# Second channel product: products in another order, scale and residual ahead of the last units, output turns into four banks

## The chip, the cores and the metric

The kernel runs on one core of a Trainium2 chip. The metric is device time in microseconds (us) of one execution of the whole program; the median of three runs is 2000.34 us (1999.61 to 2003.00). Engines are named as in the profile: PE is TensorE, PEld its weight loads, DVE is VectorE, ACT is ScalarE, POOL is GpSimd, SP is SyncE, which here only issues DMAs.

## The reference, cut to what matters

One decoder block on 512 tokens of width 2048: attention and gating heads, an output projection with a residual, then the channel MLP, and a last RMSNorm. The change lies in the last two lines.

```python
def rmsnorm(x, g):
    y = x * lax.rsqrt(jnp.mean(x * x, axis=-1, keepdims=True) + EPS)
    return y * g
...
x = x + jnp.einsum('bse,ed->bsd', merged, w_out[l])
h2 = rmsnorm(x, norm_ffn_g[l])
a = jax.nn.relu(jnp.einsum('bsd,df->bsf', h2, w_ff1[l]))   # 512 x 2048 by 2048 x 8192
x = x + jnp.einsum('bsf,fd->bsd', a * a, w_ff2[l])         # 512 x 8192 by 8192 x 2048
return rmsnorm(x, norm_final_g)
```

Since relu squared is homogeneous, the row scale of `h2` is left out of the first product and put in behind the second: the last sum is `r2 * (a * a) @ w_ff2 + x2`, where `r2` is the squared inverse root for each token and `x2` the residual.

## The kernel before, in words

Every product of two float32 matrices is computed as three matmuls in a reduced format: each operand is split into a high part (ACT, a cast into `wh`) and a low part (DVE, `wl` = operand minus `wh`), and PE adds high by high, high by low and low by high. Both channel products are blocked by two and use seven products of block sums in place of eight (the Strassen-Winograd scheme, P1 to P7).

The second channel product is `second_product`. It runs over 16 units, `(kc, n)`: eight depths `kc` of 1024, and two halves `n` of the columns. A unit has seven products; a product has two halves `h` (a group, 12 matmuls of 128x512), so a unit is 14 groups and 168 matmuls and the whole is 2688. The left factors `fac` were made by the first product, stored in DRAM and read back once per `kc` (line 877). The right factors are four blocks of `w2` per unit (B11, B12, B21, B22, each in two halves `raw`, line 870), from which DVE forms block sums in place: `B11 += B12` for P5 (line 887), `B11 += B22` for P6 (889), `B12 += B22` for P7 (891), and behind P6 `B21 += B11` for P4 (898). `prepare` (880) makes the sum, the cast (895) and the low part (896) of one group, two groups ahead of PE; `wh` and `wl` have three buffers, so a cast can start when PE has left the group three back. A block's next load is issued when its last use has been prepared (`follows`).

The products add up in PSUM where the scheme allows: P1, P6, P7 and P4 go one after the other into the pair of banks X, P2 into Y, P5 and P3 into Z. In between, the running sum in X or Z is wanted as well, so ACT copies X after P1 (`k1`), Z after P5 (`k5`) and X after P6 (`k2`) into SBUF (`keep`, line 916), a pair of copies each, and PE may not add to a bank before its copy is done. After P2, P7 and P3 DVE adds bank and kept copy into the accumulators `acc` (`add_kept`, lines 924 and 925: two additions for each half of the tokens), after P4 the bank alone (line 909).

The order of products in a unit is `usual` (P1, P2, P5, P6, P7, P3, P4); the last unit has `final`, with P4 in a pair of banks W. In the last two units (`kc` = 7) `settle` (953) scales each finished accumulator by `r2` and adds the residual (DVE, line 957), and ACT squares it and sums (959). `finish` (961), run for the first 256 tokens after P3 and for the others after P4, makes the inverse root (a short chain DVE, POOL, lines 964, 122, 123), scales the accumulators (DVE 972, ACT 970), turns them by PE into PSUM banks (981; four 128x128 turns a bank), and from each bank ACT (990) and DVE (988) take one half each, times the norm's gain, into `y`, which SP stores (991), 512 KB a time.

The order of PE's work is the order in which the code is written. That of the other engines is made by a scheduler, as is the place of a DMA in SP's queue; each queue then runs strictly in its order.

Of the kernel before, what the change touches and what calls it, by code (L numbers as in the profile page):

```python
# [8 lines left out]
F32 = mybir.dt.float32  # L9
# [25 lines left out]
def hybrid_block(ctx, tc, xT, win, wf_in, wout, w1, w2, cols_in, ln_in, ws_in, out):  # L35
# [28 lines left out]
    def mm(name):  # L64
        return ps_mm.tile([P, 512], F32, tag="mm", name=name)
# [587 lines left out]
    A11, A12, A22, S1, S2, S3, S4 = range(NF)  # L653
    P1, P2, P3, P4, P5, P6, P7 = range(1, 8)
    left = {P1: A11, P2: A12, P3: S4, P4: A22, P5: S1, P6: S2, P7: S3}
    usual = (P1, P2, P5, P6, P7, P3, P4)
    first = (P5, P1, P6, P2, P7, P4, P3)
    fac = [dram.tile([NF, P, 1024], F32, name=f"fac{u}") for u in range(NU)]
    stage = {}
# [172 lines left out]
    def second_product():  # L832
# [47 lines left out]
        def prepare(i):  # L880
            x, p, h = groups[i]

            def raw(b):
                return raws[x, b, h]

            if p == P5:
                nc.vector.tensor_tensor(raw(B11), raw(B11), raw(B12), ALU.add)
            if p == P6:
                nc.vector.tensor_tensor(raw(B11), raw(B11), raw(B22), ALU.add)
            if p == P7:  # L890
                nc.vector.tensor_tensor(raw(B12), raw(B12), raw(B22), ALU.add)
            s = raw(source[p])
            wh = w2_pool.tile([P, 1024], F32R, tag="wh", name=f"wh{x}_{p}_{h}")
            wl = w2_pool.tile([P, 1024], F32R, tag="wl", name=f"wl{x}_{p}_{h}")
            nc.scalar.copy(wh, s)  # L895
            nc.vector.tensor_tensor(wl, s, f(wh), ALU.subtract)  # L896
            if p == P6:
                nc.vector.tensor_tensor(raw(B21), raw(B21), raw(B11), ALU.add)
            ready[i] = wh, wl
            if p in follows:  # L900
                load(x + 1, follows[p], h)

        def take(bank, how):
            for t in range(2):
                how(t, bank[t])
# [10 lines left out]
                nc.scalar.copy(s[t], ps)  # L916
            return s, how

        def add_kept(c, s, first, bank, ps_op, s_op):
# [33 lines left out]
        def settle(th, q, x2l):  # L953
            a = acc[th, q]
            for t in range(2):
                tb = 2 * th + t
                nc.vector.scalar_tensor_tensor(a[:, t, :], a[:, t, :], r2[:, tb:tb + 1], x2l[:, t, :],  # L957
                                               ALU.mult, ALU.add)
                nc.scalar.activation(x2l[:, t, :], a[:, t, :], AF.Square, accum_out=sums[:, tb, q:q + 1])

        def finish(th):
            tbs = slice(2 * th, 2 * th + 2)
            r = rl[:, tbs]
            nc.vector.tensor_reduce(r, sums[:, tbs, :], axis=AX.X, op=ALU.add)
            inv_root(r, r, D, 2)
            for q in range(4):
                for t in range(2):
                    a, rt = acc[th, q][:, t, :], rl[:, 2 * th + t:2 * th + t + 1]
                    if t:
                        nc.scalar.activation(a, a, AF.Copy, scale=rt)  # L970
                    else:
                        nc.vector.tensor_scalar(a, a, rt, None, ALU.mult)
            yield 3
            for q in range(4):
                y = y_pool.tile([P, 4, 256], F32, tag="y", name=f"y{th}{q}")
                for jj in range(2):
                    ps = mm(f"pt{th}{q}{jj}")
                    for j in range(2):
                        for t in range(2):
                            c = 2 * jj + j  # L980
                            nc.tensor.transpose(ps[:, j * 256 + t * P:j * 256 + (t + 1) * P],
                                                acc[th, q][:, t, c * P:(c + 1) * P], ident)
                    for j in range(2):
                        k = 4 * q + 2 * jj + j
                        g = cols[:, G_LAST + k:G_LAST + k + 1]
                        d = y[:, 2 * jj + j, :]
                        if j:
                            nc.vector.tensor_scalar(d, ps[:, 256:512], g, None, ALU.mult)
                        else:
                            nc.scalar.activation(d, ps[:, 0:256], AF.Copy, scale=g)  # L990
                nc.sync.dma_start(out=out[q * 512:(q + 1) * 512, th * 256:(th + 1) * 256].rearrange("(m p) c -> p m c", p=P),
                                  in_=y)
# [5 lines left out]
        def evacuate(x, p):  # L998
            kc, n = units2[x]
            first, end = kc == 0, kc == LAST  # L1000
            o = order_of(x)
            name = f"{x}_{p}"
            lo, hi = 2 * n, 2 * n + 1
            X, Y, Z = banks["X"], banks.get("Y"), banks.get("Z")

            def done(c):
                if end:
                    settle(*c, x2_for[c])

            if p == P1:  # L1010
                kept[1], how = keep(f"k1_{x}")
                take(X, how)
                if end:
                    for c in ((0, lo), (0, hi), (1, hi), (1, lo)):
                        x2_for[c] = load_x2(*c)
            elif p == P2:
                add_kept((0, lo), kept[1], first, Y, ALU.add, ALU.add)
                done((0, lo))
            elif p == P6:
                kept[2], how = keep(f"k2_{x}")  # L1020
                take(X, how)
            elif p == P5:
                kept[5], how = keep(f"k5_{x}")
                take(Z, how)
            elif p == P7:
                add_kept((1, hi), kept[5], first, X, ALU.subtract, ALU.add)
                if o is final:
                    take(X, add_ps((1, lo)))
                done((1, hi))
            elif p == P3:  # L1030
                add_kept((0, hi), kept[2], first, Z, ALU.add, ALU.subtract)
                done((0, hi))
                if o is final:
# [22 lines left out]
        for i, (x, p, h) in enumerate(groups):  # L1056
# [131 lines left out]
```

## Time and profile before

| | us |
|---|---|
| median of three runs | 2000.34 |
| the profiled execution, as timed | 2002.97 |
| its span | 2001.3 |
| PE busy | 1966.3 (98%) |
| PEld busy | 1721.9 (86%) |
| DVE busy | 1597.4 (80%) |
| ACT busy | 1051.7 (53%) |

The span is the stretch from the first to the last instruction of the profiled execution; 1.7 us of the timed 2002.97 lie outside it. PE's granted clock was at its higher level (2.4 GHz) for nearly the whole span. The second channel product begins on PE at 1353.5 us and ends at 1983.5; what follows is the last norm, the turns and the stores. A matmul's end is modelled, so that PE counts as busy through short waits; its weight loads (PEld) and the distance between the starts of two matmuls show them.

### The profile page before, as it was taken

Reading aid. Unit: us, or ns where it says so; the run is one execution under the profiler, and the core shown is the slowest. Engines: PE = TensorE matmul, PEld = TensorE weight load, DVE = VectorE, ACT = ScalarE, POOL = GpSimd, SP = SyncE. Lnnn points to the kernel's source line nnn. Section 1 sums busy time; section 2 is a strip of 40 time slices with the busy share of each in tenths; the row PEclk is TensorE's granted clock in tenths of the full one; section 3 lists DMA queues with packets and bytes.
Section 4 is the critical chain, followed back from the end, with each engine's and each line's share of the span. In section 5 each row is a group of like instructions: output and inputs, shape, how many; then the busy total and the mean of one; then the engine's idle time right before and its main releaser. Section 6 shows DMA issues by size and latency. Waiting matters only on the chain.

```text
span 2001.3 us, 30641 instructions
## 1 busy us (share of the span) xinstructions
PE 1966.3 (98%) x11288; PEld 1721.9 (86%) x11288; DVE 1597.4 (80%) x2400; ACT 1051.7 (53%) x1692; POOL 84.1 (4%) x84
## 2 busy tenths in 40 slices
PE   9999999999999999999999999999999999999996
PEld 6888887888787899999999999997888888888875
DVE  7567567677667789888888888888888988998897
ACT  6344334445423566666666666666554444444455
POOL 5000001100121000000000000000000000000000
PEclk9999999999999999999999999999999999999999
DMA  6465565667766789986677667778855656646632
GB/s 217 152 198 167 186 193 174 200 211 242 247 204 199 249 270 307 334 270 201 207 243 238 209 203 236 240 263 314 328 198 202 231 165 224 241 137 237 245 128 84
DMA packets 226406, 439.91 MB, mean 220 GB/s; under 512 B 18896, under 2 KB 96848, under 8 KB 226128
## 3 DMA queue, kind: packets, MB, share of 16 engines
q1 hardware_dynamic: 225568, 436.09, 64.6%
q8 instruction: 88, 1.44, 0.3%
q10 hardware_dynamic: 432, 1.35, 0.2%
q0 software_dynamic: 256, 0.52, 0.1%
q14 instruction: 62, 0.51, 0.1%
HBM read 337.22 MB, written 100.66 MB: 219 GB/s over the span
## 4 chain that ended last, share of the span: by engine, by line
PE 58%; DVE 5%; DMA 3%; issue 1%; ACT 1%; SPq 0%; POOLq 0%; POOL 0%; DVEq 0%; ACTq 0%
PE q L802 28%; PE bX L1078 16%; PE bZ L1078 7%; PE bY L1078 4%; DMA b<-in_w_dram 1%; DVE wl L896 1%; PE ps_og L152 1%; PE ps_og L150 1%; PE ps_og L151 1%; DVE fl L734 1%; DMA x2d<-x2t 1%; DMA x2l<-x2d 0%; DVE acc L957 0%; DVE acc L924 0%; DMA t1d<-b 0%
## 5 line engine op out<-in xcount | busy, mean ns | idle before, releaser
L802 PE MATMUL q<-form,fh 128*128 128x256 f32 x3584 | 647.4, 283 | 1.0 <-DVE x L616 1.0
L802 PEld LDWEIGHTS q<-form,fh 128*128 128x128 f32 x3584 | 559.4, 192 | 1.4 <-DVE x L616 1.0
L802 PE MATMUL q<-form,fl 128*128 128x256 f32 x1792 | 508.6, 284 | 2.1 <-DVE fl L734 1.9
L895 ACT CAST wh<-raw 128x1024 fp32r<-128x1024 f32 x224 | 234.4, 1054 | 221.4 <-PE bX L1078 121.3
L802 PEld LDWEIGHTS q<-form,fl 128*128 128x128 f32 x1792 | 343.9, 192 | 4.1 <-DVE fl L734 3.4
L896 DVE TENSOR_TENSOR wl<-raw,wh 128x1024 fp32r<-128x1024 f32 x224 | 271.2, 1223 | 72.6 <-ACT wh L895 71.7
L1078 PE MATMUL bX<-wh,fac 128*128 128x512 f32 x1008 | 322.3, 393 | 4.3 <-ACT k_wl L916 2.1
L1078 PEld LDWEIGHTS bX<-wh,fac 128*128 128x128 f32 x1008 | 190.0, 188 | 52.3 <-ACT k_wh L916 6.8
L734 DVE TENSOR_TENSOR fl<-t,fh 128x512 fp32r<-128x512 f32 x256 | 176.2, 690 | 68.0 <-ACT fh L733 66.8
L733 ACT CAST fh<-t 128x512 fp32r<-128x512 f32 x256 | 158.2, 618 | 117.0 <-PE q L802 78.8
L1078 PE MATMUL bX<-wl,fac 128*128 128x512 f32 x504 | 198.8, 394 | 1.9 <-DVE wl L896 1.9
L1078 PE MATMUL bZ<-wh,fac 128*128 128x512 f32 x512 | 162.8, 389 | 0.0
L1078 PEld LDWEIGHTS bX<-wl,fac 128*128 128x128 f32 x504 | 95.0, 188 | 25.5 <-DVE wl L896 7.0
L1078 PEld LDWEIGHTS bZ<-wh,fac 128*128 128x128 f32 x512 | 96.1, 188 | 20.0
L733 ACT CAST fh<-r 128x512 fp32r<-128x512 f32 x128 | 79.1, 618 | 46.0 <-PE q L802 39.9
L150 PE MATMUL ps_qk<-xh,wh_qk 128*128 128x512 f32 x256 | 101.6, 397 | 0.0
L152 PE MATMUL ps_qk<-xh,wl_qk 128*128 128x512 f32 x256 | 100.0, 391 | 0.0
L151 PE MATMUL ps_qk<-xl,wh_qk 128*128 128x512 f32 x256 | 99.8, 390 | 0.0
L1078 PE MATMUL bZ<-wl,fac 128*128 128x512 f32 x256 | 99.6, 389 | 0.0
L734 DVE TENSOR_TENSOR fl<-r,fh 128x512 fp32r<-128x512 f32 x128 | 88.2, 689 | 10.1 <-ACT fh L733 9.4
L162 ACT ACTIVATE wh_qk<-raw_qk,cols 128x512 fp32r<-128x512 f32 x64 | 46.3, 724 | 94.7 <-PE ps_qk L151 62.9
L163 DVE SCALAR_TENSOR_TENSOR wl_qk<-raw_qk,cols,wh_qk 128x512 fp32r<-128x512 f32 x64 | 47.7, 750 | 59.0 <-ACT wh_qk L162 58.9
(618 smaller groups left out, 3559.1 us busy)
## 6 DMA issues: line engine op xcount, KB each, us to landing
b<-in_w_dram SPq DMA_DIRECT2D x256, 256.0 KB, 4.4
raw<-in_w_dram SPq DMA_DIRECT2D x128, 512.0 KB, 4.9
fac<-fac SPq DMA_DIRECT2D x112, 512.0 KB, 6.3
r<-in_w_dram SPq DMA_DIRECT2D x64, 512.0 KB, 5.6
fac<-fc SPq DMA_DIRECT2D x48, 512.0 KB, 3.9
raw_qk<-in_win_dram SPq DMA_DIRECT2D x32, 512.0 KB, 3.8
t1d<-b SPq DMA_DIRECT2D x64, 256.0 KB, 2.2
t3d<-b SPq DMA_DIRECT2D x64, 256.0 KB, 2.4
```

The lines of the kernel that those rows point to most:

```text
L150: nc.tensor.matmul(ps, lhsT=ah, rhs=bh, start=start, stop=False)
L151: nc.tensor.matmul(ps, lhsT=ah, rhs=bl, start=False, stop=False)
L152: nc.tensor.matmul(ps, lhsT=al, rhs=bh, start=False, stop=stop)
L162: nc.scalar.activation(wh, raw, AF.Copy, scale=g)
L163: nc.vector.scalar_tensor_tensor(wl, raw, g, f(wh), ALU.mult, ALU.subtract)
L733: nc.scalar.copy(pairs(wh), b[p])
L734: nc.vector.tensor_tensor(pairs(wl), b[p], pairs(f(wh)), ALU.subtract)
L802: nc.tensor.matmul(d, lhsT=l[:, c], rhs=r, start=j == 0 and q == 0 and m == 0 and w == 0, stop=j == 3 and q == 1 and w == 2, skip_group_ch ...
L895: nc.scalar.copy(wh, s)
L896: nc.vector.tensor_tensor(wl, s, f(wh), ALU.subtract)
L1078: nc.tensor.matmul(banks[chain][t], lhsT=l, rhs=r, start=start and w == 0, stop=stop and w == 2, skip_group_check=True)
```

## The change

- `usual` and `final` put P2 behind P6 instead of ahead of P5. The sum `B21 += B11` moves behind P2, and B11's next load with it. The first loads follow the new order.
- `settle` is gone. `settle_task`, started with P1 of each of the two last units, loads the four residual tiles and, before the unit's products are added, makes each accumulator `acc * r2 + x2`. The products of the two last units are then added by `add_scaled`, one instruction each, `acc + r2 * source` (or with `nr2`, which is minus `r2`). The squares (`squares`) go to ACT, and the last of the 16 to DVE as a product with a running sum.
- In `finish` the eight banks of turns of each token half alternate between the matmul pool and two banks of their own, and each bank has one reader: DVE with one instruction over both gains, or ACT with two. DVE takes five of the eight scalings in place of four. The second token half's `y` lies in buffers of `raw`, and its last 512 KB are stored in two parts.

In the rows below a name is tile, unit, product, half and a running number: `wl8_6_1` is the low part for unit 8, P6, second half; `raw8_0_1` is B11's second half (blocks 0 to 3 are B11, B12, B21, B22).

DVE, a middle unit (8), from the low part of P5's second half to that of P7's first; before:

```order
L896 TENSOR_TENSOR wl8_5_1_17744<-raw8_0_1_17492,wh8_5_1_17743 128x1024
L924 TENSOR_TENSOR acc00_15277<-acc00_15277,bY8_0_17728 128x512
L924 TENSOR_TENSOR acc00_15277<-acc00_15277,bY8_1_17729 128x512
L925 TENSOR_TENSOR acc00_15277<-acc00_15277,k1_8_wh_17719 128x512
L925 TENSOR_TENSOR acc00_15277<-acc00_15277,k1_8_wl_17720 128x512
L896 TENSOR_TENSOR wl8_6_0_17769<-raw8_0_0_17470,wh8_6_0_17768 128x1024
L898 TENSOR_TENSOR raw8_2_0_17605<-raw8_2_0_17605,raw8_0_0_17470 128x1024
L889 TENSOR_TENSOR raw8_0_1_17492<-raw8_0_1_17492,raw8_3_1_17580 128x1024
L898 TENSOR_TENSOR raw8_2_1_17623<-raw8_2_1_17623,raw8_0_1_17492 128x1024
L896 TENSOR_TENSOR wl8_6_1_17791<-raw8_0_1_17492,wh8_6_1_17790 128x1024
L896 TENSOR_TENSOR wl8_7_0_17815<-raw8_1_0_17518,wh8_7_0_17814 128x1024
```

and now:

```order
L896 TENSOR_TENSOR wl8_5_1_17707<-raw8_0_1_17491,wh8_5_1_17706 128x1024
L896 TENSOR_TENSOR wl8_6_0_17728<-raw8_0_0_17472,wh8_6_0_17727 128x1024
L889 TENSOR_TENSOR raw8_0_1_17491<-raw8_0_1_17491,raw8_3_1_17581 128x1024
L891 TENSOR_TENSOR raw8_1_1_17538<-raw8_1_1_17538,raw8_3_1_17581 128x1024
L896 TENSOR_TENSOR wl8_6_1_17747<-raw8_0_1_17491,wh8_6_1_17746 128x1024
L896 TENSOR_TENSOR wl8_2_0_17771<-raw8_2_0_17606,wh8_2_0_17770 128x1024
L898 TENSOR_TENSOR raw8_2_0_17606<-raw8_2_0_17606,raw8_0_0_17472 128x1024
L896 TENSOR_TENSOR wl8_2_1_17790<-raw8_2_1_17624,wh8_2_1_17789 128x1024
L898 TENSOR_TENSOR raw8_2_1_17624<-raw8_2_1_17624,raw8_0_1_17491 128x1024
L896 TENSOR_TENSOR wl8_7_0_17814<-raw8_1_0_17517,wh8_7_0_17813 128x1024
```

The four additions of P2 (924, 925) leave the stretch, since P2 now ends later, and the low parts of P2 and two sums for P7 (891) come into it.

ACT, the same unit, from the cast for P6; before:

```order
L895 CAST wh8_6_0_17768<-raw8_0_0_17470 128x1024
L916 COPY k5_8_wh_17809<-bZ8_0_17775 128x512
L916 COPY k5_8_wl_17810<-bZ8_1_17776 128x512
L895 CAST wh8_6_1_17790<-raw8_0_1_17492 128x1024
L895 CAST wh8_7_0_17814<-raw8_1_0_17518 128x1024
L895 CAST wh8_7_1_17837<-raw8_1_1_17537 128x1024
L916 COPY k2_8_wh_17855<-bX8_0_17685 128x512
L916 COPY k2_8_wl_17856<-bX8_1_17686 128x512
L895 CAST wh8_3_0_17859<-raw8_3_0_17562 128x1024
```

and now:

```order
L895 CAST wh8_6_0_17727<-raw8_0_0_17472 128x1024
L895 CAST wh8_6_1_17746<-raw8_0_1_17491 128x1024
L916 COPY k5_8_wh_17762<-bZ8_0_17731 128x512
L916 COPY k5_8_wl_17763<-bZ8_1_17732 128x512
L895 CAST wh8_2_0_17770<-raw8_2_0_17606 128x1024
L895 CAST wh8_2_1_17789<-raw8_2_1_17624 128x1024
L916 COPY k2_8_wh_17808<-bX8_0_17687 128x512
L916 COPY k2_8_wl_17809<-bX8_1_17688 128x512
L895 CAST wh8_7_0_17813<-raw8_1_0_17517 128x1024
```

The copies of Z (`k5`) now stand behind both casts of P6, and between the copies of X (`k2`) and P7, which adds to X, PE has P2.

DVE, the end, from the last instruction ahead of the additions of W; before:

```order
L988 TENSOR_SCALAR y01_20057<-pt011_20065,cols_112 128x256
L909 TENSOR_TENSOR acc12_15283<-acc12_15283,bW15_0_20027 128x512
L909 TENSOR_TENSOR acc12_15283<-acc12_15283,bW15_1_20028 128x512
L957 SCALAR_TENSOR_TENSOR acc12_15283<-acc12_15283,r2_151,x2l12_19808 128x512 x2
L988 TENSOR_SCALAR y02_20091<-pt020_20092,cols_112 128x256
L988 TENSOR_SCALAR y02_20091<-pt021_20099,cols_112 128x256
L988 TENSOR_SCALAR y03_20107<-pt030_20108,cols_112 128x256
L988 TENSOR_SCALAR y03_20107<-pt031_20115,cols_112 128x256
L964 TENSOR_REDUCE rl_15286<-sums_15285 128x2
L122 TENSOR_SCALAR rl_15286<-rl_15286 128x2
```

and now:

```order
L972 SCALAR_TENSOR_TENSOR acc12_15283<-bX15_1_19780,r2_151,acc12_15283 128x512
L1014 TENSOR_TENSOR y00_20059<-pt00_20060,cols_112 128x512
L1014 TENSOR_TENSOR y01_20074<-pt02_20075,cols_112 128x512
L972 SCALAR_TENSOR_TENSOR acc12_15283<-bW15_0_20045,r2_151,acc12_15283 128x512
L972 SCALAR_TENSOR_TENSOR acc12_15283<-bW15_1_20046,r2_151,acc12_15283 128x512
L1014 TENSOR_TENSOR y02_20107<-pt04_20108,cols_112 128x512
L979 ISA junk121_20105,sums_15285<-acc12_15283 128x512
L979 ISA sums_15285 128x1
L986 TENSOR_REDUCE rl_15286<-sums_15285 128x2
L122 TENSOR_SCALAR rl_15286<-rl_15286 128x2
```

Behind the additions of W (909, now 972) stood two scalings with the residual (957) and four halves of turns; now there are one whole bank of turns (1014), the last square (979, with the read of its sum) and the reduction.

The diff, cut to its core:

```diff
-    usual = (P1, P2, P5, P6, P7, P3, P4)
+    usual = (P1, P5, P6, P2, P7, P3, P4)
...
-        final = (P1, P2, P5, P6, P3, P7, P4)
+        final = (P1, P5, P6, P2, P3, P7, P4)
...
-        follows = {P6: B11, P7: B12, P3: B22, P4: B21}
+        follows = {P2: B11, P7: B12, P3: B22, P4: B21}
...
-            if p == P6:
+            if p == P2:
                 nc.vector.tensor_tensor(raw(B21), raw(B21), raw(B11), ALU.add)
...
             for t in range(2):
                 a = acc[c][:, t, :]
-                if not first:
+                if end:
+                    add_scaled(c, t, bank[t], ps_op)
+                    add_scaled(c, t, s[t], s_op)
+                elif not first:
...
+        def settle_task(n):
+
+            order = ((0, 2 * n), (0, 2 * n + 1), (1, 2 * n + 1), (1, 2 * n))
+            x2 = {c: load_x2(*c) for c in order}
+            yield 3
+            for c in order:
+                for t in range(2):
+                    a, tb = acc[c][:, t, :], 2 * c[0] + t
+                    nc.vector.scalar_tensor_tensor(a, a, r2[:, tb:tb + 1], x2[c][:, t, :], ALU.mult, ALU.add)
+                yield 1
+
+        def add_scaled(c, t, src, op):
+            a, tb = acc[c][:, t, :], 2 * c[0] + t
+            r = (nr2 if op is ALU.subtract else r2)[:, tb:tb + 1]
+            nc.vector.scalar_tensor_tensor(a, src, r, a, ALU.mult, ALU.add)
+
+        def squares(c, t, eng=None):
+            a = acc[c][:, t, :]
+            s = sums[:, 2 * c[0] + t, c[1]:c[1] + 1]
+            junk = w_pool.tile([P, 512], F32, tag="wl", name=f"junk{c[0]}{c[1]}{t}")
+            if eng is nc.vector:
+                nc.vector.tensor_tensor_reduce(junk, a, a, 1.0, 0.0, ALU.mult, ALU.add, accum_out=s)
+            else:
+                nc.scalar.activation(junk, a, AF.Square, accum_out=s)
...
-                    if t:
+                    if t and q < 3:
                         nc.scalar.activation(a, a, AF.Copy, scale=rt)
...
-                    ps = mm(f"pt{th}{q}{jj}")
+                    i = 2 * q + jj
+                    ps = ax(f"pt{th}{i}", i // 2 % 2) if i % 2 else mm(f"pt{th}{i}")
...
+                    if i in ((1, 2, 4, 6, 7) if th else (0, 2, 4)):
+                        nc.vector.tensor_tensor(d, ps.rearrange("p (j c) -> p j c", j=2),
+                                                cols[:, G_LAST + k:G_LAST + k + 2].unsqueeze(2).broadcast_to([P, 2, 256]),
+                                                ALU.mult)
+                    else:
+                        for j in range(2):
+                            nc.scalar.activation(d[:, j, :], ps[:, j * 256:(j + 1) * 256], AF.Copy,
+                                                 scale=cols[:, G_LAST + k + j:G_LAST + k + j + 1])
...
-        for p, b in ((P1, B11), (P2, B21), (P5, B12), (P6, B22)):
+        for p, b in ((P1, B11), (P5, B12), (P6, B22), (P2, B21)):
...
+            if kc == LAST and p == P1 and h == 0:
+                start_task(settle_task(n))
```

## Rows read from the trace of the kernel before

**Rows 1.** Stretches: length; busy (count) of PE, PEld, DVE, ACT, POOL; clock; DMA; GB/s.

```profile
1500.00:1600.00 100.00, 100.00 (x438) 81.47 (x437) 90.16 (x96) 45.27 (x50) 0.00 (x0) 1.00 0.61 221
...
1985.00:2002.00 17.00, 4.64 (x38) 3.84 (x36) 7.61 (x20) 7.77 (x19) 0.69 (x1) 0.87 0.65 217
```

**Rows 2.** Timeline of PE: start, length, engine, line, instruction; the second product.

```profile
1353.50 0.40 PE L1078 MATMUL bX<-wh,fac 128*128 128x512 f32 x1
...
1385.10 0.39 PE L1078 MATMUL bZ<-wh,fac 128*128 128x512 f32 x1
...
1401.42 0.39 PE L1078 MATMUL bY<-wh,fac 128*128 128x512 f32 x1
...
1417.51 0.39 PE L1078 MATMUL bX<-wh,fac 128*128 128x512 f32 x1
...
1904.17 0.39 PE L1078 MATMUL bY<-wh,fac 128*128 128x512 f32 x1
...
1943.87 0.39 PE L1078 MATMUL bY<-wh,fac 128*128 128x512 f32 x1
...
1983.46 0.39 PE L1078 MATMUL bW<-wh,fac 128*128 128x512 f32 x1
```

**Rows 3.** Timeline of all engines, unit 5, around the end of P6.

```profile
1567.87 2.00 ACT L895 CAST wh<-raw 128x1024 fp32r<-128x1024 f32 x2
...
1570.23 0.19 PEld L1078 LDWEIGHTS bX<-wl,fac 128*128 128x128 f32 x1 [0.36 <-DVE wl L896]
...
1572.38 0.59 ACT L916 COPY k_wh<-bX 128x512 f32<-128x512 f32 x1 [1.17 <-PE bX L1078]
...
1573.02 0.19 PEld L1078 LDWEIGHTS bX<-wh,fac 128*128 128x128 f32 x1 [0.42 <-ACT k_wh L916]
```

**Rows 4.** Timeline of PE, P4 of the last unit and the turns behind it.

```profile
1974.35 0.39 PE L1078 MATMUL bW<-wh,fac 128*128 128x512 f32 x1
...
1979.83 1.25 PE L981 MATMUL pt<-ident,acc 128*128 128x128 f32 x8 [1.72 <-DVE acc L909]
...
1983.69 1.91 PE L981 MATMUL pt<-ident,acc 128*128 128x128 f32 x16
```

**Rows 5.** Timeline of DVE in the last unit and behind it.

```profile
1949.71 1.28 DVE L924 TENSOR_TENSOR acc<-acc,bY 128x512 f32<-128x512 f32 x2
...
1952.11 1.41 DVE L957 SCALAR_TENSOR_TENSOR acc<-acc,r,x2l 128x512 f32<-128x512 f32 x2
1953.44 2.36 DVE L889 TENSOR_TENSOR raw<-raw,raw 128x1024 f32<-128x1024 f32 x2
...
1974.66 0.15 DVE L964 TENSOR_REDUCE rl<-sums 128x2 f32<-128x8 f32 x1
...
1983.20 1.38 DVE L909 TENSOR_TENSOR acc<-acc,bW 128x512 f32<-128x512 f32 x2
...
1987.38 0.15 DVE L964 TENSOR_REDUCE rl<-sums 128x2 f32<-128x8 f32 x1
...
1988.55 1.67 DVE L972 TENSOR_SCALAR acc<-acc,rl 128x512 f32<-128x512 f32 x4 [0.81 <-POOL rl L123]
```

**Rows 6.** Timeline of ACT behind the last product.

```profile
1988.55 2.56 ACT L970 ACTIVATE acc<-acc,rl 128x512 f32<-128x512 f32 x4 [1.23 <-POOL rl L123]
1991.02 3.01 ACT L990 ACTIVATE y<-pt,cols 128x256 f32<-128x256 f32 x8
```

**Rows 7.** Timeline of SP's queue: the first store of the second token half.

```profile
1992.41 0.37 SPq L991 DMA_DIRECT2D out_dram<-y  x1
```

**Rows 8.** Groups of DVE's instructions between 300 and 620 us: count, busy, mean ns.

```profile
L534 DVE SCALAR_TENSOR_TENSOR u<-pm,cols,u 128x512 f32<-128x512 f32 x8 | 6.0, 748 | 7.8 <-PE pm L152 7.8
...
L400 DVE TENSOR_TENSOR ptl<-pT,pth 128x384 fp32r<-128x384 f32 x3 | 1.7, 553 | 0.0
L380 DVE CUSTOM_DVE_ANT_0 p<-pS,nFk 128x384 f32<-128x384 f32 x3 | 1.6, 549 | 0.0
```

**Rows 9.** DMA issues between 1500 and 1600 us: count, size, median us to landing.

```profile
raw<-in_w_dram SPq DMA_DIRECT2D x19, 512.0 KB, 5.3
```

More of the change, by code (lines that the diff above doesn't have):

```diff
@@ L917, in keep, with add_kept @@
             return s, how
-        def add_kept(c, s, first, bank, ps_op, s_op):
+        def add_kept(c, s, first, end, bank, ps_op, s_op):
             for t in range(2):
                 a = acc[c][:, t, :]
-                if not first:
+                if end:
+                    add_scaled(c, t, bank[t], ps_op)
+                    add_scaled(c, t, s[t], s_op)
+                elif not first:
                     nc.vector.tensor_tensor(a, a, bank[t], ps_op)
@@ L933, in second_product @@
         rl = const.tile([P, NT], F32, name="rl")
+        nr2 = sm.tile([P, NT], F32, tag="rt", name="nr2")
         def load_x2(th, q):
@@ L951, in second_norm @@
             nc.vector.tensor_tensor(r2, r2, r2, ALU.mult)
[L953 to L959, printed above, removed]
+            nc.vector.tensor_scalar(nr2, r2, -1.0, None, ALU.mult)
+        def settle_task(n):
[19 more added lines that the diff above has]
+                nc.scalar.activation(junk, a, AF.Square, accum_out=s)
         def finish(th):
@@ L974, in finish @@
             for q in range(4):
-                y = y_pool.tile([P, 4, 256], F32, tag="y", name=f"y{th}{q}")
+                if th:
+                    y = raw_pool.tile([P, 2, 512], F32, tag="raw", name=f"y{th}{q}")
+                    y = y.rearrange("p a (b c) -> p (a b) c", b=2)
+                else:
+                    y = y_pool.tile([P, 4, 256], F32, tag="y", name=f"y{th}{q}")
                 for jj in range(2):
-                    ps = mm(f"pt{th}{q}{jj}")
+                    i = 2 * q + jj
+                    ps = ax(f"pt{th}{i}", i // 2 % 2) if i % 2 else mm(f"pt{th}{i}")
                     for j in range(2):
@@ L982, in finish @@
                                                 acc[th, q][:, t, c * P:(c + 1) * P], ident)
[L983 to L992, printed above, removed]
+                    k = 4 * q + 2 * jj
+                    d = y[:, 2 * jj:2 * jj + 2, :]
+                    if i in ((1, 2, 4, 6, 7) if th else (0, 2, 4)):
+                        nc.vector.tensor_tensor(d, ps.rearrange("p (j c) -> p j c", j=2),
+                                                cols[:, G_LAST + k:G_LAST + k + 2].unsqueeze(2).broadcast_to([P, 2, 256]),
+                                                ALU.mult)
+                    else:
+                        for j in range(2):
+                            nc.scalar.activation(d[:, j, :], ps[:, j * 256:(j + 1) * 256], AF.Copy,
+                                                 scale=cols[:, G_LAST + k + j:G_LAST + k + j + 1])
+                    if jj or q == 3:
+                        m = slice(0, 4) if q < 3 else slice(2 * jj, 2 * jj + 2)
+                        nc.sync.dma_start(out=out[q * 512 + m.start * P:q * 512 + m.stop * P,
+                                                  th * 256:(th + 1) * 256].rearrange("(m p) c -> p m c", p=P),
+                                          in_=y[:, m, :])
                 if q == 1:
@@ L1007, in done @@
                 if end:
-                    settle(*c, x2_for[c])
+                    for t in range(2):
+                        squares(c, t)
             if p == P1:
@@ L1012, in evacuate @@
                 take(X, how)
-                if end:
-                    for c in ((0, lo), (0, hi), (1, hi), (1, lo)):
-                        x2_for[c] = load_x2(*c)
             elif p == P2:
-                add_kept((0, lo), kept[1], first, Y, ALU.add, ALU.add)
+                add_kept((0, lo), kept[1], first, end, Y, ALU.add, ALU.add)
                 done((0, lo))
@@ L1025, in evacuate @@
             elif p == P7:
-                add_kept((1, hi), kept[5], first, X, ALU.subtract, ALU.add)
+                add_kept((1, hi), kept[5], first, end, X, ALU.subtract, ALU.add)
                 if o is final:
-                    take(X, add_ps((1, lo)))
+                    for t in range(2):
+                        add_scaled((1, lo), t, X[t], ALU.add)
                 done((1, hi))
             elif p == P3:
-                add_kept((0, hi), kept[2], first, Z, ALU.add, ALU.subtract)
+                add_kept((0, hi), kept[2], first, end, Z, ALU.add, ALU.subtract)
                 done((0, hi))
@@ L1035, in evacuate @@
             elif p == P4:
-                b = banks["W"] if o is final else X
                 if first:
-                    take(b, lambda t, ps: nc.scalar.copy(acc[1, lo][:, t, :], ps))
-                else:
-                    take(b, add_ps((1, lo)))
-                done((1, lo))
+                    take(X, lambda t, ps: nc.scalar.copy(acc[1, lo][:, t, :], ps))
+                elif end:
+                    b = banks["W"] if o is final else X
+                    for t in range(2):
+                        add_scaled((1, lo), t, b[t], ALU.add)
+                        squares((1, lo), t, nc.vector if o is final and t else None)
+                else:
+                    take(X, add_ps((1, lo)))
                 if o is final:
                     start_task(finish(1), 1)
-        x2_for = {}
-        for p, b in ((P1, B11), (P2, B21), (P5, B12), (P6, B22)):
+        for p, b in ((P1, B11), (P5, B12), (P6, B22), (P2, B21)):
             load_factor(0, p)
```

## Prediction

> **What bounds the kernel now.** I read the busy times first, then the table of stretches, then PE's timeline over the second product, all engines around one of its stalls, and last the end, engine by engine. In a middle stretch PE counts as busy for 100 of 100 us, at clock 1.00, and DVE for 90.16 [rows 1]. A learner should not stop there, since a modelled matmul end covers short waits. The starts of matmuls tell more [rows 2]: the starts at 1385.10 and 1417.51 are 143 matmuls apart in a stretch without a wait, so the pace is 32.41/143 = 0.2266 us each; a group of 12 is 2.72 us and a unit of 168 is 38.08. Against that pace the second product holds:
>
> - unit 0: 1353.50 to 1401.42 is 47.92 us for 192 matmuls (43.52): 4.40 lost
> - units 1 to 13: to 1904.17 are 502.75 us, 13 x 38.08 = 494.99: 7.76 lost, 0.60 a unit
> - unit 14: 39.70 us, 1.62 lost
> - unit 15: to 1983.46, 39.59 us for 143 steps (32.41): 7.18 lost
>
> (Units 1 to 15 are counted from the first matmul into Y, one product into the unit; the last piece therefore has 144 matmuls.) In all 20.96 us. Two waits make the 0.60 [rows 3]: at 1570.23 a weight load waits 0.36 for the low part of P6's second half, and at 1573.02, the start of P7, it waits 0.42 for ACT's copy of X. Both are ACT's order. P5 ends as P6 begins; its two copies end 0.8 later, the cast for P6's second half stands behind them (1.0), and the low part takes 1.15 to 1.2 (2.36 for two like it in [rows 5]): 3.0 to 3.1 where 2.72 is to be had. P7 adds to the bank that is copied behind P6, so the copy (0.59, begun at 1572.38) stands bare.
>
> In unit 15 the first half of P4 ends and the second starts 1980.83 - 1977.07 = 3.76 us apart: that is, the turns at 1979.83 waited 1.72 for an addition by line 909, whose bank they take over, and the rest is scaling and 16 turns [rows 4]. The other 3.4 us lie ahead of P6: DVE was behind, its additions at 1949.71, residual steps (957) at 1952.11 and only then P6's sums [rows 5].
>
> Behind the last matmul (E = 1983.46) come 3.9 us to the reduction (1987.38), 1.17 to the scalings (1988.55) [rows 5], and the first store of the second half at 1992.41, E + 8.95 [rows 7]. The stores then need 2001.3 - 1992.41 = 8.9 us.
>
> **The steady units (1 to 13).** The order removes both waits by putting a product between cause and use. In after's ACT queue the casts of P6 stand ahead of the copies of Z; behind these stand P2's, which end by P6's start + 0.8 + 1.0 + 1.2 = 3.0, where P2 begins at 5.44. The copies of X end 0.8 us after P6, and P7 begins 5.44 after it. What is late next? I walked DVE's new queue from a unit's start T: P5's low parts end at T + 2.5 and 7.0 (due 5.7 and 8.4); then P6's first, 8.5 (due 11.1), two sums (889, 891) of 1.15, and P6's second, 8.5 + 3 x 1.15 = 11.9, due at 13.8. That 1.9 is the least slack I find; P2's and P7's have 2.4 to 3.1. DVE does the same work in a unit as before, 90% of the time, so its total still fits. The moved sum B21 += B11 and B11's next load behind it lie some 5 us later in SP's queue; a load takes 5.3 us to land [rows 9], and by the walk it lands 12 us ahead of its next cast. B12 is wanted one product earlier by P5's sum, and has 11 to 14 us. So 7.76 falls to about nothing; I leave 0.3 in unit 1, where ACT may hold first-product work.
>
> Busy share and starts disagree on whether there is anything to win here. The Trainium skill, page "Perfetto Trace Analysis", section "Identifying the Most-Contended Engine", says that matmul busy time is a poor measure because matmuls are pipelined, and that the busy share of weight loads is a good one. The trace agrees: PEld shows 81.47% [rows 1], and 0.188 us of load (0.19 in [rows 3]) per 0.2266 would be 83%, so 1.5 to 2% is free; by busy share alone it would be nothing, and the sum would stop at the ends (the first rival's time).
>
> **Unit 0.** Loads come now in the order P1, P5, P6, P2, so P6's and P5's sums are wanted while DVE still empties the first product's banks. The walk makes P6's first low part end at the moment it is due, and the first B12 may land late by up to 1 us. The trace doesn't show this order, so bounds: 0 (what it waits for is off the path) and 4.4 (as now). I take 0.5, near the walk: 3.9 won.
>
> **Units 14 and 15, scaling ahead.** Before, 16 residual steps of 128x512 (957, 1.41 for two; 0.66 is the second one's share [rows 5]) stood between the products' additions. They are as many now, 16 x 0.66 = 10.6 us, but DVE's new queue has them in units 12 to 14, in DVE's idle tenth: 9.8% of 38.08 is 3.7 a unit, 11.2 over three units, which is just enough. 28 additions become scalar forms, 0.748 [rows 8] against 0.69 for an addition (1.38 for two [rows 5]): 28 x 0.06 = 1.7 us of DVE over two units. The residual loads are earlier and also 4 x 512 KB a unit as before. ACT keeps 15 of the 16 squares. So I leave 0.2 for each of units 13 to 15: 1.4 won in unit 14. In unit 15 the two parts of 7.18 go: the 3.4 ahead of P6, and of the 3.76 in P4 all but the turns. The 16 turns at 1983.69 take 1.91 to a modelled end [rows 4], 1.8 on the path. They no longer share a bank with the addition (their own two banks), and the scaling begins 0.4 us ahead of P4, takes 3 x 0.62 on ACT (2.56 for four in [rows 6]) beside 5 x 0.40 on DVE (1.67 for four [rows 5]), and is done 1.6 us into the 2.72 of P4's first half. Left: 0.2 + 1.8; won 5.2.
>
> Sum over the second product: left 0.5 + 0.3 + 0.6 + 1.8 = 3.2, won 20.96 - 3.2 = 17.8.
>
> **The end.** Behind E DVE has the two additions of W (0.66 each, at E + 0.85 and 1.5), one whole bank of turns (0.6, E + 2.15 to 2.75), the last square and the read of its sum (E + 3.55), instead of two additions, two residual steps, four half banks, and ACT's squares. No 128x512 product with a running sum is in the trace; the same kind of instruction at 128x384 takes 549 ns against 553 for an addition [rows 8], so I give it an addition's 0.65 (bounds 0.55 and 1.3, twice as much). Reduction to scaling stays 1.17: E + 4.75. ACT then has 1.86 of scaling and two halves of turns (3.01 for eight [rows 6], 0.4 each), DVE 2.0 and one bank: the first store at E + 7.5, 1.45 earlier. Bounds: E + 6.5 if DVE reaches W at once and the bank of turns is not ahead of the square, E + 9 if whole banks are slow with two gains. The stores behind it move the same 2 MB, so 8.9 stays; the last one's split is worth a few tenths at most, left out.
>
> **Total.** 17.8 + 1.4 = 19.2 us. The profiled execution took 2002.97, so its like would take 1983.8; the median of the three runs is 2.63 lower, 2000.34, and against it I forecast 2000.34 - 19.2 = 1981.2, its own range 1978.5 to 1985: 1.5 at unit 0's and the end's good sides, 4 at their bad ones. Chance 0.60.
>
> **Rivals.**
>
> 1. *The steady units give nothing.* DVE at 90.16% is the true limit, and the wait moves from P7 to P6's sums, which now come one product earlier. Then only the ends win: 3.9 + 1.4 + 5.2 + 1.4 = 11.9, so 1988.4. For it: the least slack is 1.9 us, in a queue that runs strictly in order. Against it: both waits in [rows 3] have ACT's copies behind them, and DVE's total is unchanged. 0.14.
> 2. *The first units and the last pay.* P6's sums in unit 0 come late by one transfer (5.3), or the residual steps push back the low parts of units 12 to 14, since the 11.2 us of idle DVE just hold 10.6 + 1.7. Price 3 to 6: about 1985.7. 0.14.
> 3. *It doesn't do what it says*: the stalls of unit 15 and the 0.60 come back in another place, since P5 follows P1 directly now, and both leave copies to ACT. Gain 0 to 4: 1998. 0.06.
> 4. *Slower.* A low part of P6 stands on DVE behind sums and additions whose own inputs (a bank that PE has not left, a block that has not landed) come late, and everything behind it waits in each unit. To lose the 19.2 over 16 units, it must cost 1.2 a unit, hence P6's second half must be 1.9 + 1.2 = 3.1 us later than the walk has it. At 4 us late it is 2.1 a unit, 16 x 2.1 = 33.6 against 19.2: 2014. For it: 3.7 us of idle DVE a unit could not make that good. Against it: the additions that stood there (924, 925) went elsewhere, and loads have 11 us in hand. 0.06.
>
> **Range and chances.** The forecast, the second rival and half of the first lie within 1978 to 1990, which I give; beyond are the third, the fourth and some of the ends' bounds, under 2 in 10. What a measurement can tell from no change here is about 0.2%, 4 us: faster means under 1996.3. The forecast and rivals 1 and 2 are faster, 0.88. Of the third's 0.06 I put 0.01 faster, 0.04 the same and 0.01 slower, of the fourth's 0.01 the same and 0.05 slower: faster 0.89, same 0.05, slower 0.06.
>
> **What would show it.** Right: starts of units 38.1 us apart from unit 1 on, PEld at 83% in a middle stretch, no weight load that waits for a copy at P7 or for a low part in P6; in the last unit 16 turns without a wait between the halves of P4; the first store of the second half at E + 7.5. Wrong: a weight load in P6 or P5 waiting for DVE, a unit above 38.7, unit 0 above 44, or a reduction later than E + 4.5.

## The result and the profile after

The changed kernel takes 1982.13 us (median of four runs, 1981.19 to 1983.14), where the kernel before, run beside it, takes 1999.97: ratio 0.9908, 95% interval [0.9896, 0.9921], so 16 to 21 us less. Forecast were 1981.2 us, 19.2 less. The profiled execution was timed at 1983.14 with a span of 1981.4.

PE's timeline over the second product, the answer to [rows 2] (line 1078 is now 1114): the first matmul of all, the first into Y of units 1, 13, 14 and 15, and the last of all:

```profile
1352.03 0.40 PE L1114 MATMUL bX<-wh,fac 128*128 128x512 f32 x1
...
1407.38 0.39 PE L1114 MATMUL bY<-wh,fac 128*128 128x512 f32 x1
...
1864.62 0.39 PE L1114 MATMUL bY<-wh,fac 128*128 128x512 f32 x1
...
1903.00 0.39 PE L1114 MATMUL bY<-wh,fac 128*128 128x512 f32 x1
...
1941.70 0.39 PE L1114 MATMUL bY<-wh,fac 128*128 128x512 f32 x1
...
1965.04 0.39 PE L1114 MATMUL bW<-wh,fac 128*128 128x512 f32 x1
```

From unit 1's Y to unit 13's are 457.24 us, 12 units of 38.08 and 0.28, and those 0.28 lie in unit 13 (below): units 1 to 12 hold no wait any more. The middle stretch, read as [rows 1]:

```profile
1500.00:1600.00 100.00, 100.00 (x443) 82.81 (x442) 90.96 (x95) 48.05 (x55) 0.00 (x0) 1.00 0.55 198
```

PE shows 100 of 100 as before, while its loads went from 81.47 to 82.81, as forecast (83), and the stretch has 443 matmuls in place of 438. The remaining waits, PEld in units 0, 13 and 14 (unit 15 has like ones; in 13 and 14 those of bX make nearly all of what is lost, those of bZ 0.03 each):

```profile
1363.91 0.19 PEld L1114 LDWEIGHTS bX<-wl,fac 128*128 128x128 f32 x1 [1.01 <-DVE wl L896]
```

```profile
1853.60 0.19 PEld L1114 LDWEIGHTS bZ<-wl,fac 128*128 128x128 f32 x1 [0.18 <-DVE wl L896]
1859.28 0.19 PEld L1114 LDWEIGHTS bX<-wl,fac 128*128 128x128 f32 x1 [0.38 <-DVE wl L896]
1891.97 0.19 PEld L1114 LDWEIGHTS bZ<-wl,fac 128*128 128x128 f32 x1 [0.18 <-DVE wl L896]
1897.65 0.19 PEld L1114 LDWEIGHTS bX<-wl,fac 128*128 128x128 f32 x1 [0.36 <-DVE wl L896]
```

The end, DVE's timeline behind the last matmul (against [rows 5]; line 972 is an addition with scale, 1014 a whole bank of turns, 979 the square):

```profile
1964.48 1.28 DVE L1014 TENSOR_TENSOR y<-pt,cols 128x512 f32<-128x512 f32 x2
1965.68 1.41 DVE L972 SCALAR_TENSOR_TENSOR acc<-bW,r,acc 128x512 f32<-128x512 f32 x2
1966.99 0.69 DVE L1014 TENSOR_TENSOR y<-pt,cols 128x512 f32<-128x512 f32 x1
1967.59 0.69 DVE L979 CUSTOM_DVE_ANT_0 junk<-acc 128x512 f32<-128x512 f32 x1
1968.20 0.09 DVE L979 DVE_READ_ACCUMULATOR2_ANT sums<- 128x1 f32 x1
1968.39 0.16 DVE L986 TENSOR_REDUCE rl<-sums 128x2 f32<-128x8 f32 x1
...
1969.57 2.07 DVE L994 TENSOR_SCALAR acc<-acc,rl 128x512 f32<-128x512 f32 x5 [0.81 <-POOL rl L123]
1972.13 0.69 DVE L1014 TENSOR_TENSOR y<-pt,cols 128x512 f32<-128x512 f32 x1 [0.50 <-PE pt L1008]
```

With E the start of the last matmul, 1965.04, the reduction stands at E + 3.35 (before 3.92, forecast 3.55), the first store of the second half at 1972.89, E + 7.85 (before 8.95, forecast 7.5):

```profile
1972.89 0.37 SPq L1023 DMA_DIRECT2D out_dram<-y  x1
```

PE's granted clock (the column behind the engines) at the first turns behind the scalings, before and after:

```profile
1989.09:1991.09 2.00, 2.00 (x17) 1.91 (x18) 1.13 (x3) 2.00 (x5) 0.00 (x0) 1.00 0.84 279
```

```profile
1970.11:1972.11 2.00, 2.00 (x10) 1.95 (x11) 1.53 (x4) 2.00 (x5) 0.00 (x0) 0.50 1.04 344
```

After, PE turned at its lower level (1.2 GHz), the starts of two turns 0.21 us apart in place of 0.11.

One table for all kernels: microseconds lost against 0.2267 a matmul, from the starts of the 2688 matmuls; the time from E to the span's end; and the whole from the second product's first matmul to the span's end. The last column leaves out what happens earlier: its first matmul came anywhere from 1351.2 to 1353.7 in these executions. (The end is of one execution each, and it scatters: after, rest_alone, rest_early, dose1 and dose2 have the same `finish`, and end 15.65 to 16.93 behind E. In the execution of before, a load that landed late in the first product held up PE for 1.18 us at 850.83, which the one of after doesn't have; so the two spans differ by 19.9, and by 18.4 in the part that was changed.)

| kernel | unit 0 | 1-12 | 13-14 | 15 to P4 | P4 | end | whole |
|---|---|---|---|---|---|---|---|
| before | 4.40 | 7.13 | 2.19 | 3.28 | 3.89 | 17.80 | 647.8 |
| after | 0.95 | 0.0 | 0.58 | 0.63 | 1.80 | 16.39 | 629.4 |
| order_alone | 0.92 | 0.0 | 0.0 | 3.29 | 5.90 | 17.63 | 636.8 |
| rest_alone | 4.31 | 6.57 | 5.09 | 1.90 | 1.77 | 15.66 | 644.4 |
| rest_early | 4.41 | 6.89 | 3.56 | 0.57 | 1.77 | 15.65 | 641.9 |
| old_finish | 0.78 | 0.0 | 0.63 | 0.67 | 4.00 | 15.96 | 631.1 |
| old_settle | 0.32 | 0.0 | 0.0 | 3.27 | 1.77 | 19.52 | 633.9 |
| p2_between | 1.40 | 4.06 | 0.83 | 4.08 | 3.82 | 17.71 | 641.0 |
| p3_ahead | 0.83 | 14.00 | 3.29 | 2.60 | 3.91 | 17.81 | 651.5 |
| dose1 | 1.45 | 0.0 | 1.00 | 0.68 | 1.80 | 16.13 | 630.1 |
| dose2 | 5.38 | 23.81 | 5.55 | 2.39 | 1.77 | 16.93 | 664.9 |
| tail_act | 0.71 | 0.64 | 0.62 | 0.67 | 1.80 | 15.72 | 629.2 |
| tail_dve | 0.77 | 0.0 | 0.61 | 0.67 | 1.80 | 15.85 | 628.8 |

### The profile page after: what moved, and what is told of

Its sections match the earlier page's. It is cut to its first block, busy times and chain, and to the rows that moved or that the text cites. A ratio compares the mean times of both kernels' runs of the same rounds, so it can differ in the third digit from the quotient of the medians.

```text
span 1981.4 us, 30651 instructions
## 1 busy us (share of the span) xinstructions
PE 1958.5 (99%) x11288; PEld 1724.7 (87%) x11288; DVE 1599.7 (81%) x2397; ACT 1048.9 (53%) x1688; POOL 84.6 (4%) x84
## 4 chain that ended last, share of the span: by engine, by line
PE 62%; DVE 3%; DMA 1%; issue 1%; ACT 0%; SPq 0%; DVEq 0%; POOLq 0%; POOL 0%; ACTq 0%
PE q L802 30%; PE bX L1114 16%; PE bZ L1114 8%; PE bY L1114 4%; PE ps_og L152 1%; PE ps_og L150 1%; PE ps_og L151 1%; DVE wl L896 0%; DVE acc L972 0%; DMA fac<-fac 0%; DVE fl L734 0%; PE px L646 0%; DMA b<-in_w_dram 0%; PE pt L1008 0%; DMA fac<-fc 0%
## 5 line engine op out<-in xcount | busy, mean ns | idle before, releaser
L1114 PE MATMUL bX<-wh,fac 128*128 128x512 f32 x1008 | 318.2, 389 | 0.0
L1114 PEld LDWEIGHTS bZ<-wh,fac 128*128 128x128 f32 x512 | 96.1, 188 | 19.9
```

The lines of the kernel that those rows point to most:

```text
L1114: nc.tensor.matmul(banks[chain][t], lhsT=l, rhs=r, start=start and w == 0, stop=stop and w == 2, skip_group_check=True)
```

## The experiments

Two theories stood against each other: that each gain sits at its own place (a copy, a cast or a residual step too near to its use), and that DVE, 90% busy, is the bound, so that a wait can only move. The first five kernels take the change apart.

**order_alone**, the kernel before with the new order:

```diff
-    usual = (P1, P2, P5, P6, P7, P3, P4)
+    usual = (P1, P5, P6, P2, P7, P3, P4)
... (final, follows, first loads and the sum behind P2 likewise; nothing else)
```

> The kernel before with the new order of products, first loads and follows alone; scaling, residual, squares and turns as before. My theory (gains sit at separate places and add up): the 0.60 us of units 1 to 13 goes (7.8 us), of unit 0's 4.4 some 3.5, of unit 14 about 1; unit 15 keeps the 3.76 inside P4 and something of the 3.4 ahead of P6, and the end keeps its 17.8 us behind the last matmul. Time 12 us below before, ratio 0.994. Rival (DVE is the bound, the order only moves the wait): about 2 to 4 us below before. Rival (the order is all of it): 18 us below.

1992.35 us, ratio 0.9951 [0.9935, 0.9968]; whole 11.0 less. Units 0 to 14 do what was expected, and neither rival holds. But P4 of the last unit loses 5.90 in place of 3.89, a miss: the turns now wait twice for additions on DVE, and PE then ran at its lower clock, the matmuls' starts 0.43 us apart in place of 0.23.

```profile
1967.05 0.66 PE L981 MATMUL pt<-ident,acc 128*128 128x128 f32 x4 [1.75 <-DVE acc L909]
1968.24 1.12 PE L981 MATMUL pt<-ident,acc 128*128 128x128 f32 x4 [0.54 <-DVE acc L909]
```

```profile
1969.00:1971.20 2.20, 2.20 (x7) 1.81 (x6) 2.08 (x5) 1.70 (x5) 0.00 (x0) 0.50 0.00 0
```

The second wait makes 0.6 of the 2.0 us more, the clock about 1.4.

**rest_alone**, the changed kernel with the old order. Its residual steps run behind P2's additions in the last two units, so that P2's share there is scaled twice and the sum is another one; **rest_early** starts them one group earlier (`yield 2` for `yield 3` in `settle_task`) and doesn't.

> The changed kernel with the old order of products. My theory: stalls of units 0 to 13 stay as before (4.4 and 0.60 a unit), unit 15 loses 2 of the 3.76 in P4 and most of the 3.4 ahead of P6, the end is 1.5 us shorter: 6 to 7 us below before, ratio 0.9968. Rival (the order is all of it): nothing, ratio 1.000. Rival (the early residual steps need the new order's room): unit 15 loses nothing ahead of P6, 3.5 us below before.

> As rest_alone (the changed kernel with the old order of products), with the residual steps of the last two units begun one group earlier, so that they stand ahead of P2's additions, which come earlier in the old order. My theory after rest_alone: units 0 to 12 keep their 4.4 and 0.58; the residual steps push P6's low parts back in units 13 to 15, 4 to 6 us more there than the 2.2 to be had, P4's turns win 2, and the end 2: 1 to 3 us below before, ratio 0.999. Rival (rest_alone lost its gain only because its steps stood behind P2's additions): 6 to 7 us below, 0.9968.

rest_alone: 2000.25 us, 0.9990 [0.9980, 0.9999]; rest_early: 1994.37, 0.9961 [0.9947, 0.9975], whole 5.9 less. The first expectation's sum is met only by rest_early; my own expectation for that one was too low, and its rival, that rest_alone lost its gain because its steps stood behind P2's additions, comes nearer. In both, units 0 to 12 keep the old waits, and DVE's new residual steps delay P6's low part in units 13 and 14 (rest_early, PEld):

```profile
1876.26 0.19 PEld L1114 LDWEIGHTS bX<-wl,fac 128*128 128x128 f32 x1 [1.45 <-DVE wl L896]
...
1916.20 0.19 PEld L1114 LDWEIGHTS bX<-wl,fac 128*128 128x128 f32 x1 [1.69 <-DVE wl L896]
```

Order 11.0 and rest 5.9 make 16.9 of the 18.4. By the table the missing 1.5 is the balance of three places: 2.0 in P4, which order_alone lost there; 0.8 in units 13 and 14, where the early steps cost 1.4 with the old order (3.56 against 2.19 before) and 0.6 with the new one; and about 0.9 the other way at the end, less than it scatters. So the early steps cost more where the old order left no room.

**old_finish** is the changed kernel with the old turns and ACT's square, **old_settle** the one with the old residual steps and squares.

> The changed kernel with the old turns (one pool of banks, two readers a bank, DVE four scalings) and the last square on ACT. My theory: the matmuls' waits are those of the changed kernel but for P4 of the last unit, where the turns wait again for an addition (1.5 to 2 us), and the end is 1 to 1.5 us longer: 3 us above the changed kernel, 15.5 below before, ratio 0.992. Rival (the turns lie beside the stores anyway): the end stays at 16.4 us behind the last matmul.

> The changed kernel with the old settle: the residual step stands behind each accumulator's additions, all 16 squares on ACT. My theory: units 0 to 13 as in the changed kernel (and unit 13 without its 0.3); unit 15 loses 1 to 3 us ahead of P6 or P2 on DVE, and the end gets two residual steps (1.3 us) and waits for ACT's squares: 3 to 5 us above the changed kernel, ratio to before 0.9928. Rival (residual steps are hidden in the new order wherever they stand): only the end is longer, 1.5 us above.

old_finish: 1985.11 us, 0.9918 [0.9903, 0.9932]. P4 loses 2.2 more, a little above what was expected, but the end is 0.4 *shorter* than the changed kernel's, not 1 to 1.5 longer. So a gain of the turns' new form is shown in P4 alone. That it costs 0.4 at the end is not shown: 0.4 is less than the end scatters, old_finish has the last square on ACT too, and its PE turned at the higher clock. old_settle: 1989.41, 0.9941 [0.9926, 0.9956]; 2.6 more lost ahead of P4 and 3.1 at the end. There DVE, behind with other residual steps, begins the additions of W only at E + 2.51 (after: E + 0.64), which makes 1.9; two residual steps and ACT's squares then stand before the reduction, 1.0 more:

```profile
1970.58 1.28 DVE L909 TENSOR_TENSOR acc<-acc,bW 128x512 f32<-128x512 f32 x2
1971.77 1.41 DVE L957 SCALAR_TENSOR_TENSOR acc<-acc,r,x2l 128x512 f32<-128x512 f32 x2
1973.09 0.68 DVE L992 TENSOR_TENSOR y<-pt,cols 128x512 f32<-128x512 f32 x1
1974.28 0.16 DVE L964 TENSOR_REDUCE rl<-sums 128x2 f32<-128x8 f32 x1 [0.50 <-ACT x2l L959]
```

With the old residual steps the new turns end 1.9 later than the old ones (order_alone 17.63), and win 4.1 in P4.

**Which wait is whose.** Both on the kernel before:

```diff
+    usual = (P1, P5, P2, P6, P7, P3, P4)     # p2_between
+    usual = (P1, P2, P5, P6, P3, P7, P4)     # p3_ahead; B22's next load behind P7
```

> The kernel before with P2 between P5 and P6 (P1, P5, P2, P6, P7, P3, P4). My theory (each wait is an ACT copy or cast that stands too near to its use): the 0.40 us at P6's second half goes, since the copies of Z are behind a product that doesn't need P6's casts; the 0.18 at P7's start stays, since P7 still adds to X right behind the copies: 0.18 to 0.25 a unit left, 5 us below before in units 1 to 13. Rival (DVE is what is late at P6): P6's wait stays, or moves to P2. Rival (one wait hides behind the other): P7's wait grows to 0.5.

> The kernel before with P3 ahead of P7 in every unit (P1, P2, P5, P6, P3, P7, P4), the next loads of B12 and B22 behind P7. My theory: the 0.18 us at P7's start goes and unit 0 loses its 3.5 to 4 us there; the 0.40 at P6's second half stays, since the cast still stands behind the copies of Z: 0.40 a unit left, 2.3 us below before in units 1 to 13 and 3.5 in unit 0, 6 in all. Rival (one wait hides behind the other): P6's wait grows to 0.6 and only unit 0 gains.

p2_between: 1994.04 us, 0.9961 [0.9948, 0.9974], 0.34 lost a unit; p3_ahead: 2006.55, 1.0024 [1.0015, 1.0034], 0.87 a unit, slower where 6 us less were expected. I had put 0.40 to P6 and 0.18 to P7; the two kernels show 0.24 and 0.34. With P2 between, P6's wait is gone and P7's stays as in [rows 3]:

```profile
1681.70 0.19 PEld L1078 LDWEIGHTS bX<-wh,fac 128*128 128x128 f32 x1 [0.42 <-ACT k_wh L916]
```

P2 between takes two things away at P6, ACT's copies ahead of the cast and some of DVE's work ahead of the low part, and this kernel can't tell them apart. The trace of before can (unit 5, as in [rows 3]): DVE was through with its sums and waited 0.20 us for ACT's cast, so most of the 0.24 is ACT's order, as I had said, but DVE's sums end only 0.20 earlier.

```profile
1568.95 2.36 DVE L896 TENSOR_TENSOR wl<-raw,wh 128x1024 fp32r<-128x1024 f32 x2 [0.20 <-ACT wh L895]
```

With P3 ahead of P7 the opposite holds, 0.24 stays at P6 and P7's wait is gone, but P4 now follows P7 and waits for the bank that DVE still adds from, 0.63 a unit:

```profile
1660.77 1.28 DVE L925 TENSOR_TENSOR acc<-acc,bX 128x512 f32<-128x512 f32 x2
...
1661.60 0.47 PE L1079 MATMUL bX<-wh,fac 128*128 128x512 f32 x1 [0.38 <-DVE acc L925]
```

I missed that, and also 4.4 us in unit 1. It is the same rule turned round: P3 had shielded P4 from P7's reader.

**How much room DVE has.** The changed kernel with P6's second low part formed two (dose1) or three times (dose2):

```diff
-            nc.vector.tensor_tensor(wl, s, f(wh), ALU.subtract)
+            for _ in range(2 if (p, h) == (P6, 1) else 1):      # 3 in dose2
+                nc.vector.tensor_tensor(wl, s, f(wh), ALU.subtract)
```

> The changed kernel, with the low part of P6's second half formed twice in every unit: 1.15 us more on DVE a unit, 18.4 in all, ahead of the matmuls that use it. My theory: that low part was ready 1.84 us early in units 3 to 12, so it now has 0.69, and nothing waits: same time within 0.5 us but for units 13 to 15 (up to 1 us more). Rival (DVE is the bound at 91%): 10 to 18 us more.

> The same, formed three times: 2.3 us more on DVE a unit, 36.8 in all. The third pass stands behind the low part of P2's first half in DVE's queue, so that the 1.84 us of slack are passed by 1.5 (1.84 less two passes and that low part, 3 x 1.15 = 3.45, is -1.6). My theory: P6's second half waits 1.4 to 1.6 us in each unit, 16 x 1.5 = 24 us more than the changed kernel, about 2006, all of it at that one place. Rival (DVE's sum counts, 91% + 6% still fits): nothing. Rival (DVE is the bound): 37 us more.

dose1: 1985.85 us, 0.9922 [0.9905, 0.9938], which doesn't stand clear of the changed kernel's 0.9908; whole 0.7 more, units 1 to 12 without a wait. dose2: 2020.01, 1.0090 [1.0075, 1.0105]; 35 lost more than after, nearly all at the foreseen place, 1.9 in a middle unit (1.5 expected), 4.4 and 4.9 in units 0 and 1. The stretches of dose1 and of dose2:

```profile
1500.00:1600.00 100.00, 100.00 (x443) 82.85 (x442) 94.42 (x98) 47.37 (x55) 0.00 (x0) 1.00 0.55 198
```

```profile
1500.00:1600.00 100.00, 96.82 (x426) 79.53 (x425) 91.40 (x99) 43.08 (x48) 0.00 (x0) 1.00 0.65 232
```

and PEld's wait in unit 8 of dose2:

```profile
1693.41 0.19 PEld L1115 LDWEIGHTS bX<-wl,fac 128*128 128x128 f32 x1 [2.01 <-DVE wl L897]
```

The sum, 35, is nearer to the 37 of the rival that DVE is the bound than to my 24, but that is chance: in dose2's stretch DVE is idle for 8.6 of 100 us, mostly waiting for ACT's casts, and dose1's 18.4 us more on DVE cost 0.7. At 94.42% DVE holds up nobody in these units; at 91.40%, in units that are 1.9 us longer, it costs those 1.9. The busy share alone doesn't tell the two apart, the slack at one place does.

**The end.** Both give the first two of DVE's banks of turns, 0 and 2, to ACT. tail_act also gives the last square to ACT, and bank 6, which is ACT's in the changed kernel, to DVE; tail_dve changes nothing else (its expectation counts bank 6 among DVE's, which it was not).

```diff
-                    if i in ((1, 2, 4, 6, 7) if th else (0, 2, 4)):
+                    if i in ((1, 2, 4, 6, 7) if th else (4, 6)):      # tail_act; (4,) in tail_dve
```

> The changed kernel, with the first two of DVE's banks of turns of the first token half given to ACT (DVE keeps banks 4 and 6) and the last square on ACT. My theory: DVE reaches the additions of W 0.3 us behind the last matmul in place of 0.64, nothing but the additions stands ahead of the reduction on DVE, which starts at E + 2.3 to 2.6 in place of 3.35; first store of the second half at E + 6.8 to 7.1 in place of 7.85, the end 15.4 to 15.7 us in place of 16.4; the time 0.7 to 1 us below the changed kernel, too little for the ratio to tell. Rival (ACT is late with eight half banks and the squares): reduction at E + 3.3 or later, no gain.

> The changed kernel, with the first two of DVE's banks of turns of the first token half and bank 6 given to ACT, the last square left on DVE. My theory: DVE reaches W 0.3 us behind the last matmul; then two additions, bank 4, the square and its read, reduction at E + 2.9 to 3.1; first store at E + 7.4, the end 15.9 us: half of what tail_act gives. Rival (the square, not the turns ahead of W, is what makes the reduction late): same as tail_act or the changed kernel.

tail_act: 1983.79 us, 0.9909 [0.9894, 0.9923]; tail_dve: 1982.61, 0.9902 [0.9887, 0.9916]. In both DVE is there first and waits for W (tail_act):

```profile
1964.86 1.43 DVE L972 SCALAR_TENSOR_TENSOR acc<-bW,r,acc 128x512 f32<-128x512 f32 x2 [0.23 <-PE bW L1114]
1966.21 1.33 DVE L1014 TENSOR_TENSOR y<-pt,cols 128x512 f32<-128x512 f32 x2
1967.46 0.16 DVE L986 TENSOR_REDUCE rl<-sums 128x2 f32<-128x8 f32 x1
```

The reduction comes at E + 2.35 (tail_dve 2.49), the first store at E + 6.93 (7.11), and the end is 0.7 and 0.5 us shorter than after's, less than it scatters; the reduction is the firmer sign. tail_dve shows that it was the two turns ahead of W: they alone are gone, the additions of W begin 0.9 earlier (E - 0.25) and the reduction 0.9 earlier. The rival's number (same as tail_act) came true, its reason (the square, not the turns) did not. What the square costs is not shown, since in tail_act a bank of turns stands in its place (the x2 above), against what I expected there. In the table's whole they are 0.2 and 0.6 us below the changed kernel (tail_act lost 0.64 elsewhere, in unit 1); the ratios can't tell it.

## Why the prediction was right

- *Steady units.* Right in size and cause (for P6 DVE was late nearly as ACT was, see p2_between). The walk through DVE's queue gave the slack of P6's second half as 1.9 us; the trace shows 1.84 (from the end of that low part to the matmul that uses it), for P6's first 2.67 (2.6), P2's 2.64 and 2.96 (2.4 to 3.1). One sentence was wrong: the least slack is not there but at P5's second half, 1.23; the walk had it (7.0 against 8.4) and I passed over it.
- *Unit 0.* Right in place for what is left (P6's first low part, 1363.91), 0.95 where 0.5 was taken. What the 4.40 of before were, the prediction doesn't say. The trace of before shows the second wait of the steady units there, larger: at P7 PE waits 2.55 us for ACT's second copy of X, and then about 1.6 us go to the lower clock. Both are also gone in unit 0 of p3_ahead, where P3 stands in between. Unit 1 has none of the 0.3.

```profile
1378.60 0.19 PEld L1078 LDWEIGHTS bX<-wh,fac 128*128 128x128 f32 x1 [2.55 <-ACT k_wl L916]
```

```profile
1379.60:1383.00 3.40, 3.40 (x10) 2.60 (x9) 1.16 (x1) 1.57 (x4) 0.00 (x0) 0.51 0.84 302
```

- *Units 13 to 15.* 0.58 and 0.63 left where 0.6 was taken in all. The residual steps do lie in units 12 to 14, but not wholly for nothing: order_alone and old_settle, where they stand behind the products of the last two units, lose nothing in 13 and 14. old_settle shows what they cost otherwise: 2.6 us ahead of P4 and 3.1 at the end.
- *P4.* 1.80 left, as forecast: only the turns. old_finish confirms the cause.
- *The end.* 1.41 won against 1.45, but by another sum. The reduction was 0.2 earlier than forecast; from the scaling to the first store I took 2.75 and it was 3.3, since the turns ran at granted clock 0.50 in place of 1.00 and the second bank's reader waits 0.50 us for them (rest_early, with the same code and its first turns at 1.00, needs 2.73); and the last stores took 8.5, not 8.9, which I had called a few tenths. So the match of 1.41 is luck. I credited all of it to the change of the end as a whole; old_finish against order_alone (15.96, 17.63) shows that it comes from the residual steps.
- *The sum.* 16.95 + 1.41 = 18.4 against 17.8 + 1.4 = 19.2; by the medians 17.8. The time was met within 0.9 us partly by luck, since the kernel before was 0.4 faster when run beside it.
- *Rivals.* The first (DVE the bound) and the fourth (3.1 us late on DVE) were both in reach: dose1 refutes the one, and dose2 shows that the other's mechanism is real, but needs over 1.84 us more at that place.
- *Signs.* One sign of being wrong came, loads in P5 and P6 that wait for DVE, in units 0 and 13 to 15 alone; with what they cost (0.95, 0.58, 0.63) the forecast still holds.

Left open: why dose2 waits 3.0 and 3.2 in P6 of units 0 and 1, and p3_ahead 2.1 in P2 of unit 1, where later units wait less or not at all. Much of the rest that they lose there is the clock, about 1.6 us each: behind these waits it was at 0.50 for about 3 us, the matmuls' starts 0.43 apart.

## What to carry to other kernels

Where a bank is copied or read before the next addition to it, put a product that doesn't touch it in between, and check what the product that was taken away had shielded. Read the room of a queue as the slack of each result before its use, in order of the queue, not as a busy share. Work ahead of the last step of a chain can cost as work in it does: of two turns' 1.28 us here, 0.9 came back. Read the granted clock where a stretch comes out longer than its waits.

## What was not expected of the hardware

A size: the square with running sum of 128x512 took DVE 0.69 us (modelled on the 549 ns of 128x384 in [rows 8]), the same as an addition.

And PE's granted clock, which I had left out. It fell to its lower level (0.50 or 0.51) behind waits of PE in unit 0 of before, units 0 and 1 of dose2, unit 1 of p3_ahead and P4 of order_alone, and at the last turns of after and some others. It did not fall behind every wait: ahead of its last turns PE was idle for 3.5 us in both before and order_alone, which have the same `finish`, and the first turns ran at 1.00 in the one and at 0.50 in the other. What decides is not shown.
